# One q unit instead of two in the first stage, and another split of the modulation steps between VectorE and TensorE

## The chip, the core and the metric

The kernel runs on one core of one Trainium2 chip. The metric is the device time of one execution in microseconds (us); a kernel's time is the median of its runs. Beside the runs there is one profiled execution, whose trace all views of the profile come from. PE is TensorE (matmuls), PEld its weight loads, DVE is VectorE, ACT ScalarE, POOL GpSimd, SP the engine that issues most DMAs.

## The reference, cut to what matters

One layer of a diffusion backbone on 384 tokens (128 of context, 256 latent), model width 2048, everything in float32:

```python
mod = silu(cond) @ w_ada + b_ada              # 2048 -> 6 * 2048
sh1, sc1, ga1, sh2, sc2, ga2 = split(mod, 6)
h = rmsnorm(x, norm_pre_mix) * (1 + sc1) + sh1
proj = h @ w_in          # q 512 | k 512 | v 1024 | output gate g 1024 | lr 32 | Fourier 1024
o = bidirectional gated linear attention of q, k, v, log_sigmoid(lr @ w_a2 + b), 4 heads
o = rmsnorm(o) * gla_out_norm * silu(g)
f = real(fft2(Fourier groups))
gates = sigmoid(h @ w_gate + b_gate)          # 2048 -> 4096
m = (g_a * (o @ w_br_gla) + g_b * (f @ w_br_four)) @ w_out
x = x + ga1 * rmsnorm(m, norm_post_mix)
h = rmsnorm(x, norm_pre_ffn) * (1 + sc2) + sh2
x = x + ga2 * rmsnorm((silu(h @ w_ffn_gate) * (h @ w_ffn_up)) @ w_ffn_down, norm_post_ffn)
```

`cond` is one vector for the context tokens and one for the latent ones, so `mod` is a product of a 2048 x 12288 matrix with two vectors.

## The kernel before, in words

**Exact products.** A float32 product is made of three passes in a faster format: each operand is split into a high part (`hi`, a cast on ScalarE) and the rest (`lo`, a subtraction on VectorE), and a product is hi\*hi + hi\*lo + lo\*hi. Tokens stand along the free dimension, channels on the 128 partitions: an activation is 16 tiles of 128 x 384. A weight comes in pieces of 128 x 1024 (512 KB, tile `raw`, loaded by SP), which `split` (L264) turns into `whi` and `wlo`; in most stages one such piece is a **granule**: 8 k-tiles x 3 passes = 24 matmuls of 128 x 384 (`gemm`, L322, its matmul L326). One output tile of 128 channels over 2048 inputs takes two granules (`proj`, L348). `grab` (L313) takes the oldest split weight and splits the next; about three are held ahead, in four buffers each of `whi` and `wlo`. Every engine but SP runs in the order in which the program issues its work; nothing is reordered.

**Stage A (L406 to L660).** Sixteen steps `kb`, one per k-tile of h. A step makes the first two parts of the modulation for its channels (`gemv`, L470, 16 products with two 1 MB pieces `slab` of w_ada), normalises and modulates x to h, and adds the k-tile's contribution to all of v, which is summed in six PSUM banks (`vprod`, L482, 18 matmuls of 128 x 512). It also adds the contribution to the first `XU` = 2 units of q (a unit is 128 channels): `xprod` (L506) makes three matmuls of 128 x 384 per unit into a bank (`px`, and for unit 1 the bank `pgm` of the gemv), and `flush` (L500) adds the bank to an accumulator in SBUF on VectorE. Their weights come as `xraw` (`w_x`, 128 x 256, 128 KB a step) and are split by `split_w` (L428). SP's order in a step is: the two slabs of step kb+1, `raw` of v, `xraw`. Slabs have five buffers, `raw` and `xraw` two.

**Projections (L747 to L1000).** `qk_order` (L159) is k0, k1, then the q units that stage A has not made (q1 is made in stage A when XU is 2), then k2, k3: the first is `proj` with modulation steps alone beside it, the others with `side()`. Then come `GF` = 25 units of the merge gates. After each granule `side()` runs one step of the attention generator `gla()` and one **modulation step**. `gla` treats the heads one after another; a head is 14 steps (a step ends at a `yield`), of which one for each direction makes the exponentials and `qi`, `ki`, `ko` (L830 to L868) and the next makes the products `at` (L875) from them. Head 0 has three empty steps more.

**Modulation steps.** Three of the other four parts of the modulation are made by `ada_rest` (L685), in six groups of 18 steps: 16 k-steps, one empty step, and one that sums over partitions on TensorE (L718); the rest of that one (`ada_tail`, L665: two transposes and a few small VectorE operations) runs at the start of the next group's first k-step. A k-step has POOL load 512 KB (`adaw`, two buffers) and then multiplies it by the two conditioning columns: on VectorE with two operations of 128 x 1024 into `adacc` (L707, or L705 in a group's first), or, if `on_pe[0]` is set, on TensorE with eight matmul instructions into a bank `pr` (L697), called a TensorE granule of the modulation.

**Output gates and branches (L1000 to L1310).** After the Fourier projections comes `mix_order`: eight output-gate units `o` (two granules each, then `gcol`, L1193), the Fourier branch units `b` (`four`, L1225; one behind the third `o`, then one between the granules of each further `o` and one behind it), then sixteen branch units `a` of the attention branch (one granule each, from L1282) with five `b` among them. A `b` needs its weights folded by two VectorE operations (`fold`, L239) ahead of the cast and the subtraction. In the output gates `side()` (L1179) is called after each granule; call it turn 0 to 15. In before a modulation step is made at turns 0 to 8, 9, 11, 13, 15, on TensorE from turn 7 on but for turn 8. Ahead of the branch units `a` in `TAIL` (L41) one step is made, on TensorE where the entry is True. VectorE makes for each `a` the two merge operations L1296 and L1297 and the split of the one before (L379). The stage after, the output projection (L1350), needs all sixteen.

**The rest.** The output projection with the last steps of `ada_rest`, two norms, and the FFN with the last part of the modulation, where pieces of 128 x 512 are multiplied (L338), take from 733 us to the end.

The lines that set the modulation steps in the output gates and the branch units:

```python
on_pe[0] = turn[0] > 6 and turn[0] != 8      # side(), L1181
if turn[0] < 9 or turn[0] % 2:
    next(ada_gen, None)
...
if i in TAIL:                                # branch unit a, L1286
    on_pe[0] = TAIL[i]
    next(ada_gen, None)
```

Of the kernel before, what the change touches and what calls it, by code (L numbers as in the profile page):

```python
# [25 lines left out]
T = TC + TL  # L26
# [8 lines left out]
FC = 4  # L35
NFC = FT // FC
G = 1024
XU = 2
GF = 25
GD = 256  # L40
TAIL = {1: True, 4: False, 5: True, 8: True, 10: False, 11: True, 13: True, 14: False, 15: False}  # L41


C_TRI = 0
# [63 lines left out]
def tile_step(ctx: ExitStack, tc: tile.TileContext, a, o):  # L108
# [302 lines left out]
    with ExitStack() as s:  # L411
# [54 lines left out]
        pgm = pss.tile([P, 512], F32, tag="side", name="pgm")  # L466
        pgv, pmod = pgm[:, 0:256], pgm[:, 256:512]
        px = pss.tile([P, T], F32, tag="side", name="px")
# [10 lines left out]
        def passes(w):  # L479
            return ((0, w[0]), (0, w[1]), (1, w[0]))  # L480
# [25 lines left out]
        def xprod(u, kb, w, bank=px):  # L506
            def mm():
                for j, (x_, w_) in enumerate(passes(w)):
                    PE.matmul(bank, w_[:, u * P : (u + 1) * P], hT[x_][:, kb, :], start=j == 0, stop=j == 2)  # L509

            return mm, lambda dst=None: flush(xacc[u], kb == 0, dst, bank)
# [38 lines left out]
        prev = None  # L550
        for kb in range(KT):
            if kb and kb + 1 < KT:
                load_slab(kb + 1)
                load_w(kb + 1)
                if kb == 4:
                    load_later()

            wait = kb in (1, 2)
            if kb and not wait:
                gemv(kb)  # L560
            todo = []
            if kb > 4 and kb % 4 == 2:
                todo.append(lrprod(kb - 6))

            both = kb > 2
            if both:
                xs = [xprod(u, kb - 1, prev[1], bank) for u, bank in enumerate((px, pgm[:, 0:T]))]
            elif kb:
                todo += [xprod(u, kb - 1, prev[1]) for u in range(XU)]
            todo += [None] * (4 - len(todo))  # L570
            flushes = [t[1] if t else lambda: None for t in todo]

            def pe_x(n):
                if todo[n]:
                    todo[n][0]()

            if wait:
                vprod(kb - 1, prev[0], (0,))
            pe_x(0)
            hf = scr[:, kb % 8, :]  # L580

            xr = hf if kb else qs[0]
            DVE.tensor_mul(xr, xn(kb), rstd if kb else px)
            flushes[0]()
            if wait:
                gemv(kb)
            if kb:
                ev = pb.tile([P, 256], F32, tag="ev", name="ev")
                ACT.copy(ev, pgv)
            lag = []  # L590
            new = split_w(kb, lag)
            if kb:
                vprod(kb - 1, prev[0], (1 if wait else 0,))
            for m in range(2):
                PE.transpose(pmod[:, m * P : (m + 1) * P], ev[:, m * P : (m + 1) * P], ident)
            if kb == 0:

                for _ in range(6):
                    PE.matmul(pv[5][:, 0:P], ones, ones, start=True, stop=True)
            pe_x(1)  # L600

            pm = pb.tile([P, 2, 2], F32, tag="pm", name="pm", bufs=2)
            DVE.tensor_reduce(
                pm, pmod.rearrange("p (m q r) -> p m r q", m=2, q=4)[:, :, 0:2, :], axis=mybir.AxisListType.X, op=ALU.add,
            )
            DVE.tensor_scalar(
                mods[:, 1, kb, :], pm[:, 1, :], bsc1[:, 0, kb : kb + 1], norms[:, 0, kb : kb + 1],
                op0=ALU.add, op1=ALU.mult,
            )
            DVE.tensor_scalar_add(mods[:, 0, kb, :], pm[:, 0, :], cols[:, 0, kb : kb + 1])  # L610
            for lo, hi, c in segs:
                DVE.tensor_scalar(
                    hf[:, lo:hi], xr[:, lo:hi], mods[:, 1, kb, c : c + 1], mods[:, 0, kb, c : c + 1],
                    op0=ALU.mult, op1=ALU.add,
                )
                if kb == 0:
                    ACT.activation(
                        hT[0][:, kb, lo:hi], xr[:, lo:hi], AF.Identity,
                        bias=mods[:, 0, kb, c : c + 1], scale=mods[:, 1, kb, c : c + 1],
                    )  # L620
            flushes[1]()
            if kb:
                split_act(hT[0][:, kb, :], hT[1][:, kb, :], hf)
            else:
                ACT.copy(rstd, px)
                DVE.tensor_sub(hT[1][:, kb, :], hf, hT[0][:, kb, :].bitcast(F32))
            if kb:
                if not wait:
                    vprod(kb - 1, prev[0], (1,))
                pe_x(2)  # L630
                flushes[2]()
            if both:
                for mm, _ in xs:
                    mm()
                for _, fl in reversed(xs):
                    fl()
            for sub in lag:
                sub()
            if kb:
                vprod(kb - 1, prev[0], (2,))  # L640
                pe_x(3)
                flushes[3]()
            prev = new
# [109 lines left out]
    with ExitStack() as s:  # L753
# [25 lines left out]
        def gla():  # L779
# [10 lines left out]
            for h in range(NH):  # L790
# [38 lines left out]
                for d in range(2):  # L829


                    bT = pss.tile([P, T], F32, tag="side", name="bT")
                    for t in range(3):
                        for j, l in enumerate((lah, lal)):
                            PE.matmul(
                                bT[:, t * P : (t + 1) * P], l[:, t, d], tri[:, d * P : (d + 1) * P],
                                start=j == 0, stop=j == 1,
                            )
                    sx = pss.tile([P, 2, P], F32, tag="side", name="sx")
                    for j, l in enumerate((lah, lal)):  # L840
                        PE.matmul(
                            sx, tri[:, (2 + d) * P : (3 + d) * P], l[:, 0 : 2 + d : 1 + d, d], start=j == 0, stop=j == 1,
                        )
                    eb = pg.tile([P, T], F32, tag=f"eb{d}", name="eb")
                    ACT.activation(eb, bT, AF.Exp)
                    ki = pg.tile([P, T], F32, tag=f"ki{d}", name="ki")
                    ACT.activation(ki, bT, AF.Exp, scale=-1.0)
                    ko = pg.tile([P, 2, P], F32, tag=f"ko{d}", name="ko")
                    ACT.activation(ko, sx, AF.Exp)
                    qi = pg.tile([P, T], F32, tag=f"qi{d}", name="qi")  # L850
                    DVE.scalar_tensor_tensor(qi, eb, DK**-0.5, qT[:, h, :], op0=ALU.mult, op1=ALU.mult)
                    DVE.tensor_mul(ki, ki, kT[:, h, :])
                    DVE.tensor_mul(ko, ko, krs[:, 0 : 2 + d : 1 + d, :])

                    last = 0 if d else CH - 1
                    tot = chunks(eb)[:, :, d, last : last + 1]
                    kc = pg.tile([P, 3, CH], F32, tag=f"kc{d}", name="kc")
                    DVE.tensor_mul(kc, chunks(ki)[:, :, d, :], tot.to_broadcast([P, 3, CH]))
                    dc = pg.tile([P, 1], F32, tag=f"dc{d}", name="dc")
                    c = 5 if d else 2  # L860
                    e0, e1 = c * CH + last, (c + 1 - 2 * d) * CH + last
                    DVE.tensor_mul(dc, eb[:, e0 : e0 + 1], eb[:, e1 : e1 + 1])
                    qin.append(qi)
                    kin.append(ki)
                    kcr.append(kc)
                    kout.append(ko)
                    dec.append((tot, dc))
                    yield  # L868

                ats = []  # L870
                for d in range(2):
# [33 lines left out]
                ap = [apt[:, 0], apt[:, 1]]  # L905
                split_act(*ap, att)
                yield
                qpt = [pg.tile([P, 2, 3, P], F32R, tag=t, name="qp") for t in ("lah", "lal")]
                qp = [[q[:, d] for q in qpt] for d in range(2)]
                for d in range(2):  # L910
# [88 lines left out]
    px = fs.enter_context(tc.tile_pool(name="px", bufs=1))  # L999
# [93 lines left out]
    with ExitStack() as s:  # L1093
# [83 lines left out]
        turn = [0]  # L1177

        def side():  # L1179
            while True:  # L1180
                on_pe[0] = turn[0] > 6 and turn[0] != 8  # L1181
                if turn[0] < 9 or turn[0] % 2:
                    next(ada_gen, None)
                on_pe[0] = False
                turn[0] += 1
                next(df, None)
                next(nw, None)
                yield
# [121 lines left out]
    with ExitStack() as s:  # L1310
# [94 lines left out]
        u = pd.tile([P, 2, 3], F32, name="u12", bufs=1)  # L1405
# [355 lines left out]
        bank = {}  # L1761
# [69 lines left out]
        for kind, c, i in steps[:-4]:  # L1831
# [8 lines left out]
            if kind == "D":  # L1840
# [9 lines left out]
                h = hid_last if last_c else hid  # L1850
# [248 lines left out]
```

## Time and profile before

| what | us |
|---|---|
| median of 3 runs | 1943.53 (1941.89 to 1943.78) |
| profiled execution, device time | 1942.28 |
| profiled execution, span from first to last instruction | 1940.4 |

About 1.9 us lie around the span. TensorE's granted clock was 0.998 of full speed over the span. In the profile page the first part gives the busy time of each engine, the second the span in 40 slices, the fourth the chain of work that ended last; the groups, the waits, the windows and the timeline are views of the same trace that can be asked for a stretch of it. A time such as 612.53 is us from the span's start. A matmul's end is modelled and overlaps the next one's start, so the cost of a run of matmuls is read from start to start.

### The profile page before, as it was taken

How to read it: one execution, taken by the hardware profiler on the slowest of the kernel's cores; microseconds unless marked ns; L12 is line 12 of the kernel's file. 1: busy time of each engine (PE TensorE's matmuls, PEld its weight loads, DVE VectorE, ACT ScalarE, POOL GpSimd, SP SyncE). 2: the span in 40 equal slices, each digit the busy share in tenths (PEclk: the TensorE clock that was granted, in tenths of full speed). 3: DMA queues.
4: the chain of work that ended last, by engine and by line, in shares of the span. 5: the costliest groups of instructions: out<-in, count | busy, mean ns of one | idle time of the engine just before them, and what ended most of it. 6: DMA issues, size and time to landing. Idle time of an engine off the chain costs nothing.

```text
span 1940.4 us, 27538 instructions
## 1 busy us (share of the span) xinstructions
PE 1920.4 (99%) x10534; PEld 1690.8 (87%) x10534; DVE 1647.8 (85%) x2172; ACT 916.3 (47%) x1298; POOL 85.8 (4%) x154
## 2 busy tenths in 40 slices
PE   9999999999999999999999999999999999999997
PEld 5779999999999999999988888888888888888886
DVE  5668898889878887978789888999998999888885
ACT  4235455545456554456455444444444444444444
POOL 0001111100000000104000000000000000000001
PEclk9999999999999999999999999999999999999999
DMA  9977766766757885755264636363636272625243
GB/s 390 387 260 248 240 234 227 248 231 194 225 185 246 302 302 181 245 193 198 83 195 131 200 103 194 121 211 98 216 104 213 91 222 93 201 76 185 87 173 110
DMA packets 200615, 380.52 MB, mean 196 GB/s; under 512 B 14196, under 2 KB 126932, under 8 KB 196132
## 3 DMA queue, kind: packets, MB, share of 16 engines
q1 hardware_dynamic: 181252, 320.84, 48.9%
q0 software_dynamic: 13952, 50.39, 8.5%
q10 hardware_dynamic: 5280, 7.55, 1.1%
q8 instruction: 82, 1.34, 0.3%
q14 instruction: 49, 0.40, 0.1%
HBM read 361.94 MB, written 16.78 MB: 195 GB/s over the span
## 4 chain that ended last, share of the span: by engine, by line
PE 93%; DVE 3%; DMA 2%; issue 1%; ACT 1%; SPq 0%; DVEq 0%; ACTq 0%
PE pgu L338 30%; PE pmm L326 30%; PE pdn L338 18%; PE pv L491 3%; PE pgm L474 1%; PE pf L1239 1%; PE pfo L1039 1%; DVE adacc L707 1%; PE pmm L1516 1%; PE ptr L1808 1%; PE pf L1240 1%; PE pfo L1040 1%; DMA xraw<-in_w_x 1%; PE po L788 1%; PE px L509 0%
## 5 line engine op out<-in xcount | busy, mean ns | idle before, releaser
L326 PE MATMUL pmm<-A_hi,whi 128*128 128x384 f32 x1072 | 361.7, 337 | 0.0
L326 PE MATMUL pmm<-A_hi,wlo 128*128 128x384 f32 x1072 | 358.8, 335 | 0.0
L326 PE MATMUL pmm<-A_lo,whi 128*128 128x384 f32 x1072 | 358.6, 335 | 0.0
L1663 ACT CAST whi<-u 128x1024 fp32r<-128x1024 f32 x200 | 210.6, 1053 | 281.5 <-DVE u L1647 86.5
L1663 ACT CAST whi<-raw 128x1024 fp32r<-128x1024 f32 x175 | 184.2, 1052 | 200.8 <-PE pgu L338 63.8
L1674 DVE TENSOR_TENSOR wlo<-u,whi 128x1024 fp32r<-128x1024 f32 x200 | 244.1, 1220 | 32.0 <-ACT whi L1663 18.3
L338 PE MATMUL pgu<-whi,A_hi 128*128 128x512 f32 x640 | 250.0, 391 | 0.0
L338 PE MATMUL pgu<-whi,A_lo 128*128 128x512 f32 x640 | 249.3, 389 | 0.0
L1674 DVE TENSOR_TENSOR wlo<-raw,whi 128x1024 fp32r<-128x1024 f32 x175 | 213.4, 1220 | 34.6 <-ACT whi L1663 25.6
L287 DVE TENSOR_TENSOR wlo<-raw,whi 128x1024 fp32r<-128x1024 f32 x163 | 198.2, 1220 | 24.1 <-ACT whi L300 23.7
L300 ACT CAST whi<-raw 128x1024 fp32r<-128x1024 f32 x149 | 156.0, 1051 | 117.6 <-PE pmm L326 50.0
L326 PEld LDWEIGHTS pmm<-A_hi,whi 128*128 128x128 f32 x1072 | 201.2, 188 | 3.3 <-issue 2.5
L326 PEld LDWEIGHTS pmm<-A_lo,whi 128*128 128x128 f32 x1072 | 201.4, 188 | 0.2
L326 PEld LDWEIGHTS pmm<-A_hi,wlo 128*128 128x128 f32 x1072 | 201.2, 188 | 0.3 <-DVE wlo L287 0.2
L707 DVE SCALAR_TENSOR_TENSOR adacc<-adaw,spad,adacc 128x1024 f32<-128x1024 f32 x160 | 198.1, 1279 | 3.5 <-DMA adaw<-in_w_ada 3.2
L338 PE MATMUL pdn<-whi,hid_hi 128*128 128x512 f32 x480 | 186.9, 389 | 0.0
L338 PE MATMUL pdn<-whi,hid_lo 128*128 128x512 f32 x480 | 186.8, 389 | 0.0
L338 PE MATMUL pgu<-wlo,A_hi 128*128 128x512 f32 x640 | 184.2, 389 | 0.0
L338 PEld LDWEIGHTS pgu<-whi,A_hi 128*128 128x128 f32 x640 | 120.2, 188 | 26.1 <-issue 0.8
L338 PEld LDWEIGHTS pgu<-wlo,A_hi 128*128 128x128 f32 x640 | 120.1, 188 | 25.4
L338 PEld LDWEIGHTS pgu<-whi,A_lo 128*128 128x128 f32 x640 | 120.1, 188 | 25.0
L338 PE MATMUL pgu<-whi,S 128*128 128x512 f32 x480 | 131.1, 395 | 0.0
(405 smaller groups left out, 3042.7 us busy)
## 6 DMA issues: line engine op xcount, KB each, us to landing
adaw<-in_w_ada POOLq DMA_DIRECT2D x96, 512.0 KB, 4.0
raw<-in_w_d SPq DMA_DIRECT2D x88, 512.0 KB, 3.7
slab<-in_w_ada SPq DMA_DIRECT2D x32, 1024.0 KB, 10.2
raw<-in_w_gate SPq DMA_DIRECT2D x64, 512.0 KB, 4.4
raw<-in_w_g SPq DMA_DIRECT2D x48, 512.0 KB, 3.4
raw<-in_w_u SPq DMA_DIRECT2D x48, 512.0 KB, 3.5
raw<-in_w_in SPq DMA_DIRECT2D x44, 512.0 KB, 4.3
u<-in_w_u SPq DMA_DIRECT2D x40, 512.0 KB, 4.6
```

The lines of the kernel that those rows point to most:

```text
L287: eng.tensor_sub(lo, raw, hi.bitcast(F32))
L300: ACT.copy(hi, raw)
L326: PE.matmul(dst, w[wi][:, k * n + n0 : k * n + n0 + P], x[xi][:, k0 + k, :], start=first and k == 0 and j == 0, stop=last and k == kts - 1 ...
L338: PE.matmul(dst, stat[x_][m], mov(w[w_], m), start=first and w_ == m == x_ == 0, stop=last and w_ == m == 1,)
L474: PE.matmul(pgv[q : q + 32, :], spad[:, k, :], slab[k // (KT // 2)][:, k % (KT // 2), :], start=k < 4, stop=k >= KT - 4,)
L491: PE.matmul(pv[2 * t + g], hT[x_][:, kb, t * P : (t + 1) * P], w_[:, g * 512 : (g + 1) * 512], start=kb == 0 and j == 0, stop=kb == KT - 1 ...
L707: DVE.scalar_tensor_tensor(acc[:, c, :], w, spad[:, k, c : c + 1], acc[:, c, :], op0=ALU.mult, op1=ALU.add,)
L788: PE.matmul(dst, w[wi], x[xi], start=first and j == 0, stop=last and j == 2)
L1039: PE.matmul(p, w_of[0][:, i, k, g, :], x[:, :, lo:hi], start=kt == 0, stop=False)
L1040: PE.matmul(p[:, 0], w_of[1][:, i, k, g, :], x[:, 0, lo:hi], start=False, stop=kt == KT - 1)
L1663: ACT.copy(hi, src)
L1674: DVE.tensor_sub(lo, src, hi.bitcast(F32))
```

## The change

```diff
-XU = 2
+XU = 1
-TAIL = {1: True, 4: False, 5: True, 8: True, 10: False, 11: True, 13: True, 14: False, 15: False}
+TAIL = {1: False, 3: False, 5: False, 7: False, 8: False, 10: False, 13: False, 14: False, 15: False}
...
-                xs = [xprod(u, kb - 1, prev[1], bank) for u, bank in enumerate((px, pgm[:, 0:T]))]
+                xs = [xprod(u, kb - 1, prev[1], bank) for u, bank in enumerate((px, pgm[:, 0:T])[:XU])]
...                                              # gla(), after the loop that makes qi, ki, ko
+                if h == 0:
+                    yield
...                                              # gla(), after the splits of att
+                if h == 0:
+                    yield
...                                              # side() of the output gates
-                if turn[0] < 9 or turn[0] % 2:
+                if turn[0] < 7 or turn[0] in (8, 9, 13, 15):
                     next(ada_gen, None)
```

Stage A makes one unit of q; its `xraw` is 128 x 128. The unit q1 becomes one more `proj` in the projections, behind k1: two granules, two calls of `side()`. Head 0 of the attention gets two more empty steps, one ahead of `at` and one ahead of the products of the new states. The number of modulation steps up to the end of the branch units is the same (87): two more beside the projections, two fewer in the output gates, nine in the branch units as before. With the two steps more ahead of them, the steps of the generator fall on other turns: turns 3 and 4 become the empty step and the sum of a group, turn 5 the tail and the next group's first k-step, turns 6 and 8 its second and third. On TensorE are turns 9, 13 and 15 alone (five in the output gates and five in the branch units before); VectorE makes all nine steps in the branch units (four before). From the output projection on nothing differs.

## The prediction

> **What bounds the kernel now.** I read the page's busy times and chain first, then the busy time of each engine by stage.
>
> ```profile
> PE 1920.4 (99%) x10534; PEld 1690.8 (87%) x10534; DVE 1647.8 (85%) x2172; ACT 916.3 (47%) x1298; POOL 85.8 (4%) x154
> PE 93%; DVE 3%; DMA 2%; issue 1%; ACT 1%; SPq 0%; DVEq 0%; ACTq 0%
> ```
>
> ```profile
> core 0: us, PE busy (x) PEld busy (x) DVE busy (x) ACT busy (x) POOL busy (x), PEclk, DMA share, GB/s
> 44.00:128.00 84.00, 84.00 (x662) 60.45 (x661) 52.86 (x125) 23.62 (x44) 0.00 (x0) 1.00 0.96 366
> 160.00:195.00 35.00, 33.45 (x227) 33.03 (x226) 33.95 (x39) 21.72 (x30) 3.96 (x8) 1.00 0.68 233
> ...
> 583.00:657.00 74.00, 74.00 (x493) 70.31 (x486) 63.57 (x131) 49.08 (x74) 3.17 (x6) 1.00 0.79 257
> 657.00:727.00 70.00, 70.00 (x436) 66.87 (x435) 60.67 (x108) 35.63 (x62) 3.68 (x7) 1.00 0.90 313
> ```
>
> TensorE makes the time: it is busy in 99% of the span, and 93% of the chain is PE. So an edit is worth the matmul time that it takes away, plus the stalls of TensorE that it ends, less those that it makes. The windows say where new ones threaten. In stage A (44 to 128) TensorE has no gap, but the DMA engines are busy for 0.96 of the time as well. Where the first attention head runs (160 to 195), VectorE is the busier engine, 33.95 of 35 us, and TensorE misses 1.55 us. In the output gates (583 to 657) and the branch units (657 to 727) VectorE is busy for 63.57 of 74 and 60.67 of 70 us: it is a close second, and the change sends it work there.
>
> **Stage A gives up one unit of q.** These are pieces of the chain, start and length:
>
> ```profile
> 26.33 0.23 PE pgm L595 x2
> ...
> 28.03 0.52 ACT A_hi L378
> ...
> 105.65 1.86 PE pgm L474 x32
> ...
> 111.23 0.52 PE pgm L509 x3
> ...
> 113.14 1.86 PE pgm L474 x32
> ```
>
> ```profile
> 242.50 8.32 PE pmm L326 x48
> ```
>
> A step takes 113.14 - 105.65 = 7.49 us, without a gap. Unit 1 (`pgm`) is 0.52 of it, so 16 steps give 16 x 0.523 = 8.4 us. Its 48 matmuls come back as two granules in the projections, 8.32 us there (8.35 with the change of granule). On matmuls alone the move is worth nothing. I take two amounts off the gain. Step 1 does not get shorter: from its transposes (26.33) to the cast (28.03) that TensorE waits for runs a chain of small VectorE operations, and the dropped unit lies beside it, 0.5 us. The other amount is in the transfers:
>
> ```profile
> 20.00:40.00 20.00, 19.51 (x158) 12.71 (x157) 12.59 (x28) 6.72 (x13) 0.00 (x0) 1.00 1.02 415
> ```
>
> ```profile
> slab<-in_w_ada SPq DMA_DIRECT2D x26, 1024.0 KB, 9.8
> raw<-in_w_v SPq DMA_DIRECT2D x14, 512.0 KB, 5.8
> ```
>
> ```profile
> 60.13 0.61 PEld L474 LDWEIGHTS pgm<-slab,spad 128*32 128x32 f32 x16 [0.25 <-DMA slab<-in_w_ada]
> ```
>
> With `xraw`, 128 KB by the code, a step reads 2 x 1024 + 512 + 128 KB = 2.75 MB, afterwards 2.69 MB. At the 415 GB/s of the window from 20 to 40 us that is 6.63 and 6.47 us against 7.49 and 6.97 us of TensorE: in the steady state TensorE stays the bound. The start does not have that room. At 60.13 (step 6) the weight load waits 0.25 us for its slab, so this slab lands just in time; by then TensorE is to be four shorter steps earlier (2.1 us), the transfers only 5 or 6 x 0.16 us. I take a stall of 1.2 us. Stage A: -8.4 + 0.5 + 1.2 = **-6.7**, between -8.4 (no wait) and -2.5 (16 x 64 KB at 415 GB/s: the transfers as the bound throughout). I take a value nearer the first end because the wait at 60.13 is no longer than 0.25 us and ends within its step. With the two granules: **+1.7** (0 to +5.9).
>
> The Trainium skill, "DMA: Bandwidth & Descriptors", section Specifications, gives about 358 GB/s as the HBM limit of one core; by it a step of 2.69 MB could not take less than an estimated 7.5 us, stage A would gain nothing, and the sum below would be some 7 us higher. The row above shows 415 GB/s, so the trace does not agree, and that case stands only as a rival, on its own rows.
>
> **The first head.** Its products `at` wait for VectorE.
>
> ```profile
> PEld at L875 <- issue: 1.7, 1, 1.7
> PE at L875 <- DVE ki L852: 1.5, 1, 1.5
> ```
>
> With the new empty step a granule of 4.2 us lies between `ki` and `at`, while VectorE needs only one more modulation step and one subtraction, 2.4 + 1.1 us (rows below). The stall goes: **-1.7** (end to end 0, if it comes back at another wait for VectorE, which is then 1.7 us further behind). Next is the subtraction `wlo` of the granules, which has granules in hand.
>
> **Seven modulation steps go from TensorE to VectorE.** First TensorE, two starts that follow each other:
>
> ```profile
> 590.58 0.64 PE L697 MATMUL pr<-adaw,spad 128*32 128x256 f32 x8
> 591.15 0.55 PE L1196 MATMUL pt<-ident,qk 128*128 128x128 f32 x3
> ```
>
> A step costs TensorE 0.57 us; seven fewer are 4.0 us. Two of the seven land beside the projections, where a granule of 8.32 / 2 = 4.16 us leaves room for a step and a subtraction of VectorE, 2.4 + 1.1 us: nothing to pay, but up to 2.4 us of lag if the head's own work fills that room. Five come into the branch units. Now VectorE:
>
> ```profile
> 586.39 1.23 DVE L287 TENSOR_TENSOR wlo<-ws,whi 128x1024 fp32r<-128x1024 f32 x1 [1.11 <-ACT whi L294]
> ...
> 591.80 0.23 DVE L676 COPY mods<-ptm 128x8 f32<-128x8 f32 x2
> ...
> 592.33 0.61 DVE L1199 SCALAR_TENSOR_TENSOR gs<-gs,gnorm,pt 128x384 f32<-128x384 f32 x1
> ...
> 599.88 1.41 DVE L705 TENSOR_SCALAR adacc<-adaw,spad 128x1024 f32<-128x1024 f32 x2
> 601.21 1.22 DVE L287 TENSOR_TENSOR wlo<-ws,whi 128x1024 fp32r<-128x1024 f32 x1
> ```
>
> ```profile
> 675.46 2.47 DVE L707 SCALAR_TENSOR_TENSOR adacc<-adaw,spad,adacc 128x1024 f32<-128x1024 f32 x2
> 677.85 0.68 DVE L243 TENSOR_TENSOR ws<-raw 128x512 f32<-128x512 f32 x1
> ```
>
> From start to start a step costs 677.85 - 675.46 = 2.39 us, a group's first 601.21 - 599.88 = 1.33, the tail 592.33 - 591.80 = 0.53. What VectorE has more to do from turn 5 to the last branch unit: at turn 5 tail and first step stand ahead of an output gate, whose other operands come later by the sum that turn 4 now makes on TensorE, and push it back some 1.2 us (an estimate from 0.53, 1.33 and the sum's 1.0); at turn 6 a step, of which 1.11 fills the wait at 586.39: 1.28; at turn 7 the tail is gone: -0.53; at turn 8 a full step in place of a first one: 1.06; in the branch units nine steps for four: 5 x 2.39 = 11.95. Together **15.0 us**. Against it stands VectorE's idle time, of which only that spent waiting for TensorE can be used up:
>
> ```profile
> DVE wlo L287 <- ACT whi L294: 6.6, 9, 1.2
> ```
>
> ```profile
> DVE gate L1296 <- PE pmm L326: 8.5, 9, 1.5
> ```
>
> The first is the output gates (583 to 657): VectorE waits there for casts of its own results, and these waits move with it. The second is the branch units (657 to 728): 8.5 us that it can use. So its last split for the branch units comes 15.0 - 8.5 = 6.5 us later. When is it needed?
>
> ```profile
> 736.47 1.23 DVE L379 TENSOR_TENSOR A_lo<-yb,A_hi 128x384 fp32r<-128x384 f32 x2
> ```
>
> ```profile
> 737.58 0.33 PE L326 MATMUL pmm<-A_hi,whi 128*128 128x384 f32 x1
> ```
>
> It ends at 737.7. The output projection's second granule starts with k-tile 8 at 737.58 and gets to k-tile 15 after 21 matmuls of 8.32 / 48 = 0.173 us, at 741.2: 3.6 us in hand. TensorE gets there 6.5 - 3.6 = 2.9 us later than now instead of 4.0 earlier. I take **+2.8**: the saving is lost and more. The ends are -4.0 (VectorE is never waited for) and +6 (the late merges also hold PSUM banks, and late subtractions hold the `raw` buffers that SP must refill, as it already waits for VectorE there).
>
> **The sum.** +1.7 - 1.7 + 2.8 = +2.8 us. On the profiled execution, 1942.3 (span 1940.4 and 1.9 around it), that is 1945.1; this execution is 1.2 below the median of the runs, so I set the sum on the median: 1943.5 + 2.8, or **1946** rounded down. A measurement of this kernel can tell about 0.2%, 3.9 us, from no change.
>
> **The rivals.**
> *VectorE hides it all* (faster). The lead of the granules and the idle time carry the nine steps, and stage A gains in full: -8.4 + 8.35 - 1.7 - 4.0 = -5.8, 1938. For it: TensorE waits for VectorE hardly anywhere now. Against it: 15.0 us of work on 8.5 us of idle time and 3.6 us in hand.
> *Stage A is bound by transfers* (slower). If TensorE's shorter step meets DMA engines that cannot go faster, the step shrinks only by its bytes, 2.5 us over the stage: +5.9 - 1.7 + 2.8 = +7, 1950.5. It decides once 2.69 MB take longer than 6.97 us, below 386 GB/s. For it: a DMA share of 0.96 and 366 GB/s; against it: 415 GB/s in the stretch where the transfers set the pace.
> *A lagging VectorE costs more than its own work* (slower): banks and `raw` buffers as above, +6 in place of +2.8: 1949.5.
> *The stall of head 0 only moves* (it does not do what it says): +4.5, 1948.
>
> **Chances.** Forecast 0.50, its own range 1943 to 1949 (0.40 of it within 3.9 us, 0.10 above); VectorE hides it 0.13 (0.11 faster, 0.02 same); transfers 0.17 (slower); more lag 0.15 (0.11 slower, 0.04 same); moved stall 0.05 (0.03 same, 0.02 slower). Faster 0.11, same 0.49, slower 0.40. For 8 in 10 the range leaves out most of the first rival and the upper half of the transfers': 1940 to 1950.5.
>
> **What would show it.** Right: steps of 6.97 us in stage A with one longer wait for a slab near step 6; no wait of `at` for `ki`; no idle time of VectorE before L1296 from 660 to 725, and waits of TensorE for `wlo` or `A_lo` between 595 and 745 of 6 to 7 us in all. Wrong: steps near 7.4 us (transfers), or TensorE without a gap up to 745 (VectorE hides it). Past 745 both kernels do the same, and a difference there would be none of these.

## The result and the profile after

The changed kernel takes 1945.23 us (median of 22 runs, 1943.46 to 1946.31), the kernel before 1942.61 us beside it (22 runs, 1941.39 to 1944.13). The ratio is 1.0013 with a 95% interval of 1.0007 to 1.0019: 2.6 us slower (1.4 to 3.7), less than the 0.2% named in the prediction. The profiled execution took 1945.94 us, its span is 1944.2 us.

The engines' busy times and the chain, from the page of the changed kernel:

```profile
PE 1918.4 (99%) x10478; PEld 1690.7 (87%) x10478; DVE 1655.8 (85%) x2172; ACT 915.6 (47%) x1301; POOL 85.8 (4%) x154
PE 81%; DVE 8%; DMA 5%; ACT 2%; issue 2%; SPq 0%; ACTq 0%; DVEq 0%
```

TensorE has 2.0 us less to do than before, yet the span is longer: VectorE's part of the chain grew from 3% to 8%, that of DMA from 2% to 5%. The windows that were read before show where (columns as there: busy time of PE, PEld, DVE, ACT, POOL, then clock, DMA share and GB/s):

```profile
44.00:128.00 84.00, 83.19 (x671) 58.01 (x664) 48.66 (x121) 23.95 (x47) 0.00 (x0) 1.00 0.93 360
160.00:195.00 35.00, 35.00 (x237) 34.68 (x236) 33.41 (x38) 19.06 (x26) 4.47 (x10) 1.00 0.67 235
583.00:657.00 74.00, 72.88 (x465) 69.76 (x464) 64.91 (x125) 47.14 (x72) 2.64 (x5) 1.00 0.73 235
657.00:727.00 70.00, 66.67 (x389) 66.02 (x388) 69.18 (x117) 35.92 (x62) 3.17 (x6) 0.98 0.90 302
```

Stage A has a gap of 0.8 us of TensorE. The gap of the first head (1.55 us before) is gone. In the output gates TensorE misses 1.1 us and in the branch units 3.3 us, where it missed nothing before, and VectorE, which had 9.3 us without work in the branch units, is now busy in 69.18 of 70 us.

**Stage A.** The chain in the steady part, start and length of each piece:

```profile
108.66 1.86 PE pgm L474 x32
110.53 1.58 PE pv L491 x6
112.11 0.22 PE pgm L595 x2
112.33 1.39 PE pv L491 x6
113.72 0.52 PE px L509 x3
114.25 1.39 PE pv L491 x6
115.63 1.86 PE pgm L474 x32
```

A step takes 115.63 - 108.66 = 6.97 us, with TensorE alone in the chain: unit 1 is gone from it, and no transfer has taken its place. At step 6 a transfer does: the weight load for the second half of the gemv waits for its slab, 1.29 us in the place of 0.25. (At step 3, 37.36 us, it waits 0.98 us in the place of 0.23.)

```profile
59.31 0.59 PEld L474 LDWEIGHTS pgm<-slab,spad 128*32 128x32 f32 x16 [1.29 <-DMA slab<-in_w_ada]
```

**Output gates and branches.** The waits of TensorE from 595 to 745 us, in all, times, longest:

```profile
PE pf L1244 <- DVE wlo L287: 4.5, 4, 1.9
```

All four are at Fourier units (`b`), whose folded weights need two VectorE operations more than others before the subtraction. The lag is thus paid there, and not, as forecast, at the output projection. The last splits for the branch units:

```profile
742.60 1.22 DVE L379 TENSOR_TENSOR A_lo<-yb,A_hi 128x384 fp32r<-128x384 f32 x2
```

742.60 against 736.47 before. In this execution TensorE is late enough by then not to wait for them.

One thing in this trace was in no forecast, the clock right behind the longest of the four waits:

```profile
705.00:706.00 1.00, 0.99 (x4) 0.99 (x5) 1.00 (x1) 0.00 (x0) 0.00 (x0) 0.65 0.94 322
706.00:708.00 2.00, 2.00 (x9) 2.00 (x9) 1.97 (x5) 0.82 (x2) 0.00 (x0) 0.50 0.92 322
708.00:709.00 1.00, 1.00 (x7) 1.00 (x6) 1.00 (x2) 1.00 (x3) 0.00 (x0) 0.65 0.79 268
```

The granted clock is 0.50 from 706 to 708 and, by 0.65 in the windows beside it, for 0.7 us more on either side: 3.4 us at half rate, which cost TensorE 1.7 us.

### The profile page after: what moved, and what is told of

The parts are those of the page before. It is cut to its first block, busy times and chain, and to the rows that moved or that the text cites. A ratio compares the mean times of both kernels' runs of the same rounds, so it can differ in the third digit from the quotient of the medians.

```text
span 1944.2 us, 27444 instructions
## 1 busy us (share of the span) xinstructions
PE 1918.4 (99%) x10478; PEld 1690.7 (87%) x10478; DVE 1655.8 (85%) x2172; ACT 915.6 (47%) x1301; POOL 85.8 (4%) x154
## 4 chain that ended last, share of the span: by engine, by line
PE 81%; DVE 8%; DMA 5%; ACT 2%; issue 2%; SPq 0%; ACTq 0%; DVEq 0%
PE pgu L338 29%; PE pmm L326 25%; PE pdn L338 17%; PE pv L491 2%; DMA slab<-in_w_ada 2%; DVE adacc L707 2%; DVE wlo L287 1%; DMA raw<-in_w_in 1%; PE pgm L474 1%; PE pfo L1043 1%; PE pmm L1520 1%; DVE wlo L1678 1%; DMA raw<-in_w_g 1%; ACT whi L300 1%; PE ptr L1812 1%
## 5 line engine op out<-in xcount | busy, mean ns | idle before, releaser
L326 PE MATMUL pmm<-A_hi,whi 128*128 128x384 f32 x1088 | 366.8, 337 | 0.0
L326 PE MATMUL pmm<-A_hi,wlo 128*128 128x384 f32 x1088 | 364.2, 335 | 0.5 <-DVE wlo L287 0.5
L326 PE MATMUL pmm<-A_lo,whi 128*128 128x384 f32 x1088 | 363.9, 334 | 0.0
L707 DVE SCALAR_TENSOR_TENSOR adacc<-adaw,spad,adacc 128x1024 f32<-128x1024 f32 x174 | 215.4, 1280 | 3.7 <-DMA adaw<-in_w_ada 3.3
```

The source lines that it names most:

```text
L326: PE.matmul(dst, w[wi][:, k * n + n0 : k * n + n0 + P], x[xi][:, k0 + k, :], start=first and k == 0 and j == 0, stop=last and k == kts - 1 ...
L707: DVE.scalar_tensor_tensor(acc[:, c, :], w, spad[:, k, c : c + 1], acc[:, c, :], op0=ALU.mult, op1=ALU.add,)
```

## The experiments

All times are medians beside runs of the kernel before on the same chip; the latter had medians of 1942.5 to 1942.7 us. A difference of medians is known to about 1.7 us, so the small terms are read from the traces, by the start of the same instruction in each.

### The changed kernel again

No edit.

> The changed kernel once more, in another execution. Three things of its first trace are to be told apart: what belongs to the change and what to one execution. Theory: the waits of TensorE for folded branch weights (L1244 for wlo, 4.5 us between 595 and 745) recur, as does the wait for a slab near step 6 of stage A; VectorE is busy without a gap from 660 to 737 (76.18 of 77 us in the first trace). Rival: the half-rate stretch of TensorE's clock behind the 1.86 us wait at 705 (0.50 between 706 and 708), the 0.64 us wait at 521 and the later 0.8 us in the FFN belong to the change too, and recur. I expect these three to be absent or elsewhere, and 2 to 3 us over the kernel before as the time; with all of them again it would be 3.7.

Measured: 1945.15 us against 1942.51 (+2.6; ratio 1.0014, 1.0005 to 1.0023), span 1942.2 us. Its waits of TensorE from 595 to 745 us:

```profile
PE pf L1244 <- DVE wlo L287: 4.4, 4, 1.8
PE pmm L326 <- DVE A_lo L379: 0.8, 1, 0.8
```

and the branch units in it, with the last splits (the first row is a window):

```profile
660.00:737.00 77.00, 73.67 (x435) 73.02 (x435) 76.14 (x122) 35.66 (x62) 4.22 (x8) 1.00 0.90 302
```

```profile
741.76 1.22 DVE L379 TENSOR_TENSOR A_lo<-yb,A_hi 128x384 fp32r<-128x384 f32 x2
```

The waits at the Fourier units recur, so does that for the slab (1.6 us). The clock stays at 1.00 this time, although the same wait, 1.85 us, precedes: the half-rate stretch belongs to an execution. Two more runs below execute the changed program from the projections on and have the same wait of 1.85 us at this place: with more bytes the clock falls (0.50 from 720 to 722 us), with the small loads later it does not. The wait at 521 is absent too. And with TensorE 1.7 us earlier, the forecast wait at the output projection is there: TensorE waits 0.8 us for `A_lo` at k-tile 14 (741.2 us). From the last merge gate to the FFN this execution takes 412.0 us, the one with the half rate 412.3; the other two take 411.8 us without and 412.3 with it. So most of the 1.7 us that the clock took away, TensorE would otherwise have spent waiting for VectorE, which sets the end of this stretch.

### TAIL of before on the changed kernel

```diff
-TAIL = {1: False, 3: False, 5: False, 7: False, 8: False, 10: False, 13: False, 14: False, 15: False}
+TAIL = {1: True, 4: False, 5: True, 8: True, 10: False, 11: True, 13: True, 14: False, 15: False}
```

> The changed kernel with TAIL of before: five of the nine modulation steps in the branch units are on TensorE again, everything else as changed. Theory (VectorE's work sets the branch units): VectorE has 15.0 - 11.95 = 3.05 us more to do than before against 8.5 us of usable idle time, so the waits for folded weights at 686 and 703 go and VectorE waits for TensorE in the branch units again; the waits at 598 to 627 (1.6 us in all, ahead of any step of TAIL) stay. Against before: +1.7 - 1.7 - 1.1 (two steps fewer on TensorE) + 1.6 = +0.5 us, some 2 us under the changed kernel. First rival (the waits in the output gates are made up later): -1.1. Second rival (the loss is not in the branch units): five steps of 0.57 us more on TensorE and no wait less, changed kernel + 2.9, +5.5 against before.

Measured: 1942.99 us against 1942.51 (+0.5; ratio 1.0003, 0.9994 to 1.0012). Waits of TensorE from 595 to 745, then of VectorE from 657 to 741:

```profile
PE pf L1244 <- DVE wlo L287: 1.1, 2, 0.7
```

```profile
DVE gate L1300 <- PE pmm L326: 4.9, 4, 1.5
```

The theory's number, though the interval (-1.2 to +2.3 us) would hold the first rival's as well; the trace decides. VectorE again waits for TensorE in the branch units, and the two waits at 612 and 627 us, ahead of any step of `TAIL`, stay. From the last merge gate to the FFN this kernel takes 410.7 us, 0.6 more than the kernel before: two steps fewer on TensorE give 1.35 us, and the two waits take 1.94 us from start to start, 0.8 more than the idle time in the row. So the rest of the loss lies in the five steps, and more than the two steps of the output gates save is lost in the output gates themselves.

### Six on VectorE, three on TensorE

```diff
-TAIL = {1: False, 3: False, 5: False, 7: False, 8: False, 10: False, 13: False, 14: False, 15: False}
+TAIL = {1: True, 3: False, 5: True, 7: False, 8: True, 10: False, 13: False, 14: False, 15: False}
```

> The changed kernel with three of the nine steps in the branch units on TensorE (units 1, 5, 8), six on VectorE. Theory: VectorE has 15.0 - 3 x 2.39 = 7.8 us more to do than before, which the 8.5 us of usable idle time just hold; its last split for the branch units comes no later than before, TensorE keeps 4 of the 7 saved steps (2.3 us). Against before: 0 - 2.3 + 1.6 (the waits at 598 to 627) = -0.7 us, the fastest of the three splits. Rival (what costs is each late subtraction, not the sum of VectorE's work): waits at the Fourier units stay in part, 1 to 2 us, and the time is that of before or up to +1.3.

Measured: 1943.15 us against 1942.51 (+0.6; ratio 1.0003, 0.9994 to 1.0012). The time does not tell it from the run before. In the trace no wait of TensorE for VectorE is left between 628 and 745 us, and from the last merge gate to the FFN it takes 409.2 us, 0.9 less than the kernel before (410.1) and 1.5 less than with `TAIL` of before (410.7), as the theory has it; but a wait of 0.8 us at 521 us, which is ahead of the edit, and two waits in the FFN's last pieces near 1890 us (1.3 us, 0.4 in the kernel before) took the gain away. The trace speaks for the theory; the time leaves it open.

### Nine on VectorE, on the kernel before

```diff
-TAIL = {1: True, 4: False, 5: True, 8: True, 10: False, 11: True, 13: True, 14: False, 15: False}
+TAIL = {1: False, 3: False, 5: False, 7: False, 8: False, 10: False, 13: False, 14: False, 15: False}
```

> The kernel before with one edit alone: TAIL of the change, nine steps in the branch units on VectorE in place of four. Theory by the sum of VectorE's work: 11.95 us more against 8.5 us of idle time, so its last split comes 3.45 us later, 741.2 instead of 737.7, and TensorE, 2.85 us ahead of before at that place (5 x 0.57), waits for it until the time at which it is there now: no difference, 0 (-0.5 to +0.5). Rival one (VectorE hides the five steps): -2.85. Rival two (the five steps bring the whole loss of the change, by waits at the Fourier units that add up): +2 to +3.

Measured: 1941.74 us against 1942.51 (-0.8; ratio 0.9992, 0.9983 to 1.0001). TensorE's waits from 595 to 745, and the last splits:

```profile
PE pf L1240 <- DVE wlo L287: 1.4, 1, 1.4
PE pmm L326 <- DVE A_lo L379: 0.8, 1, 0.8
```

```profile
739.20 1.22 DVE L379 TENSOR_TENSOR A_lo<-yb,A_hi 128x384 fp32r<-128x384 f32 x2
```

```profile
L1296 DVE TENSOR_TENSOR gate<-gate,pmm 128x384 f32<-128x384 f32 x16 | 8.8, 549 | 0.0
```

The last row is a group of VectorE from 657 to 741 us; its last number is the idle time ahead of it, 8.5 us before and none now. So the five steps used up 8.5 us and made the last splits 739.20 - 736.47 = 2.7 us later: 11.2 us, 2.24 us a step and not the 2.39 of the row in the prediction. The 0.75 us between these 2.7 and the 3.45 us of the expectation is the size of the miss from 0 to -0.8. By the medians alone -0.8 is not told from 0 (-3.3 to +0.2 us); the trace has 409.35 us from the last merge gate to the FFN against 410.14. Nine steps are a small gain here, and a loss in the change, since there VectorE comes to the branch units 2.6 us later (its first merge at 659.6 in the second execution of the changed kernel, 656.9 before).

### An empty step of head 0 alone

```diff
                     dec.append((tot, dc))
                     yield
+                if h == 0:
+                    yield
```

> The kernel before with one empty step of head 0 ahead of the products at, nothing else. Theory: at no longer waits 1.5 us for ki and the time of the first head falls by 1.7 us, -1.7 against before; by this the unit of q moved out of stage A is worth +1.7 of the change's 0 up to the end of the projections. Rival (the wait only moves to another product of the same head, or to the end of the attention, where one step more is drained behind the projections): 0.

Measured: 1944.19 us against 1942.73 (+1.5; ratio 1.0008, 0.9999 to 1.0017). The theory's -1.7 falls; a loss by the medians is likely, not certain (-0.2 to +3.3 us). No wait of `at` is left, but these came; TensorE's waits from 140 to 445 us, then from 445 to 480:

```profile
PE dl L788 <- DVE part L379: 0.4, 1, 0.4
PE bT L835 <- DVE lal L379: 0.4, 1, 0.4
```

```profile
PE pmm L326 <- DVE wlo L287: 1.5, 1, 1.5
```

The attention now has one step more than before, and the calls of `side()` are the same 60: at the end of the projections three steps are drained at once instead of two, VectorE does them ahead of the next subtraction, which starts at 445.84 us where it started at 444.27, and TensorE waits for a later one at 458 us. The change does not have this wait: q1 brings two granules and so two calls more for its two empty steps. That is the cover under which the stall of head 0 could go.

The other half of the miss is the size of that stall. The kernel before and the two kernels that differ from it only behind 650 us are three executions of one program there:

```profile
PE at L875 <- DVE ki L852: 1.5, 1, 1.5
```

```profile
PE at L875 <- DVE ki L852: 0.7, 1, 0.7
```

```profile
PE at L875 <- DVE ki L852: 0.3, 1, 0.3
```

(the kernel before, nine steps, eight steps). With the pause around the wait that is 1.7, 0.9 and 0.5 us: the first trace showed the largest.

### Eight on VectorE, on the kernel before

```diff
-TAIL = {1: True, 4: False, 5: True, 8: True, 10: False, 11: True, 13: True, 14: False, 15: False}
+TAIL = {1: False, 3: False, 5: False, 7: False, 8: True, 10: False, 13: False, 14: False, 15: False}
```

> The kernel before with eight steps in the branch units on VectorE in place of four (unit 8 alone on TensorE). The run with nine gave -0.8 us, with VectorE's work 11.2 us longer up to its last split, 2.23 us a step. Theory by the sum: 4 x 2.23 = 8.9 us more against 8.5 us of idle time and 3.6 us in hand, so the last split comes in time and TensorE keeps 4 x 0.57 us: -2.3. Rival (each late subtraction of a Fourier unit counts by itself): a wait of 1 to 1.6 us at the Fourier unit near 700 stays, as with nine, and the time is -0.7 to -1.3.

Measured: 1939.99 us against 1942.73 (-2.7; ratio 0.9989, 0.9980 to 0.9998). It beats both kernels. The window of the branch units:

```profile
657.00:727.00 70.00, 70.00 (x421) 69.34 (x420) 69.21 (x113) 34.84 (x60) 3.69 (x7) 1.00 0.91 316
```

TensorE has no gap and VectorE almost none. From the last merge gate to the start of the output projection it takes 195.6 us, 198.6 before: 3.05 us for four steps, 0.76 each and not 0.57. Where the rest comes from, the starts around such a step of the kernel before show:

```profile
692.79 0.34 PE L326 MATMUL pmm<-o_hi,wlo 128*128 128x384 f32 x1
693.06 0.64 PE L697 MATMUL pr<-adaw,spad 128*32 128x256 f32 x8
693.62 0.45 PE L326 MATMUL pmm<-o_hi,whi 128*128 128x384 f32 x1
693.91 0.34 PE L326 MATMUL pmm<-o_lo,whi 128*128 128x384 f32 x1
694.09 0.35 PE L326 MATMUL pmm<-o_hi,wlo 128*128 128x384 f32 x1
```

From 692.79 to 694.09 three matmuls at 0.173 us would take 0.52 us; with the step it is 1.30. The step costs 0.78: the matmul ahead of it and the one behind it are 0.10 and 0.12 us longer from start to start, which the row used for the forecast (from the step's first start to the next) left out.

### Both edits together

```diff
+                if h == 0:
+                    yield                  # ahead of at
...
+TAIL = {1: False, 3: False, 5: False, 7: False, 8: True, 10: False, 13: False, 14: False, 15: False}
```

> The two edits together, the empty step of head 0 and eight steps on VectorE, on the kernel before, with two units of q in stage A. Theory: the terms lie in different stages and add up, -1.7 - 2.3 = -4.0 us. Rival: one of them is given back at a later wait, -1.7 to -2.3.

Measured: 1942.18 us against 1942.73 (-0.6; ratio 0.9999, 0.9991 to 1.0008). 2.2 us more than with eight steps alone: the wait of 1.5 us at 458 is there again, and one of 1.1 us at 521. Within what the medians can tell the terms do add up, but that of the empty step is a loss.

### The empty step moved, not added

Two kernels, each with eight steps on VectorE and the empty step ahead of `at`, and one of the other three empty steps of head 0 taken away: one of the two behind the splits of `la`, or the one ahead of `z`.

```diff
                 if h == 0:
                     yield
-                    yield                  # the first kernel, behind the splits of la
...
-                if h == 0:                 # the second kernel, ahead of z
-                    yield
```

> The kernel before with eight steps in the branch units on VectorE, and in head 0 one of the two empty steps behind the splits of la moved to the place ahead of at, so that the attention has as many steps as before. Theory: the wait of at for ki (0.5 to 1.7 us in the three executions of this program up to there) goes, and with no step added at the end of the attention the wait of 1.7 us near 458 does not come: about 1 us under the run with eight steps alone, -3.7 against before. Rival: the sums bT of head 0, now one granule earlier, wait for lal, and the gain is given back: -2.7 or less of a gain.

> As the run with the moved empty step, but the step taken away is the empty one at the start of head 0, ahead of the product z. Theory: the same, -3.7 against before, no wait of at for ki and none near 458. Rival: z or the splits of la, one granule earlier, wait instead: -2.7 or less of a gain.

Measured: 1940.32 us against 1942.48 (-2.2; 0.9986, 0.9977 to 0.9995) and 1941.33 us (-1.1; 0.9991, 0.9982 to 0.9999), neither under the 1939.99 of the eight steps alone (-2.7 beside its own runs of the kernel before). For the first the interval, -4.5 to -1.0 us, still holds the theory's -3.7; the traces decide. TensorE's waits from 140 to 445 us, one row of each:

```profile
PE dl L788 <- DVE part L379: 1.3, 1, 1.3
```

```profile
PE z L808 <- ACT krs L796: 1.3, 1, 1.3
```

`at` waits no longer and the end of the attention is as before, but now the products of the states wait for a split, or `z` for ScalarE's copy of `krs`. The rival is right, at another place than it had named in the first kernel: with as many granules as before, head 0's stall was moved, and not ended, by both places tried.

### More bytes in stage A

```diff
             SP.dma_start(xraw[kb], a["w_x"][kb])
+            more = pb.tile([P, G], F32, tag="more_x", name="more_x", bufs=1)
+            SP.dma_start(more, a["w_gate"][kb, 0])
```

> The changed kernel with 512 KB more read in every step of stage A (a piece that nothing uses), 3.19 MB a step in place of 2.69 MB. Theory: stage A has room in its transfers, whose limit is near the 415 GB/s of the window from 20 to 40 us; 3.19 MB take 7.7 us there, so the steady step grows from 6.97 to about 7.7 us and the stage by 9 to 11 us. First rival (the transfers are the bound of the changed stage already, at 2.69 MB in 6.97 us, 386 GB/s): every byte counts, steps of 8.3 us, 18 to 21 us more. Second rival (the limit is far above 415 GB/s): steps stay below 7.2 us, less than 4 us more.

Measured: 1959.44 us, one run, 14.2 us over the changed kernel. Starts of gemv steps, and a window over five of them:

```profile
112.68 1.07 PE L476 MATMUL pgm<-slab,spad 128*32 128x256 f32 x16
...
120.43 1.07 PE L476 MATMUL pgm<-slab,spad 128*32 128x256 f32 x16
122.07 1.07 PE L476 MATMUL pgm<-slab,spad 128*32 128x256 f32 x16 [0.57 <-DMA slab<-in_w_ada]
```

```profile
89.00:128.00 39.00, 36.40 (x284) 24.43 (x283) 20.83 (x52) 10.15 (x20) 0.00 (x0) 1.00 1.02 413
```

The steady step is 120.43 - 112.68 = 7.75 us, with a wait for a slab in each, at 413 GB/s and a DMA share of 1.02: the theory's 7.7 us. So the limit of the transfers is where the window from 20 to 40 us showed it, and the changed stage, with 2.69 MB in 6.97 us (386 GB/s), lies under it. The Trainium skill ("DMA: Bandwidth & Descriptors", section Specifications) gives about 358 GB/s for one core, as half of what two cores share; with the one core that runs here, this run does not agree with that figure as a limit. The stage grew by 13.5 us, more than the 9 to 11 expected: steps 1 to 6 lost 8.6 of these. The start had no room; besides, the clock was 0.50 from 68 to 70 us behind a wait of 2.1 us, and the added piece has one buffer, so that SP waited for it (24.4 us in all from 40 to 130 us). What each of the three cost is not separated.

### Four small loads later

```diff
         def load_later():
             SP.dma_start(wlr, a["w_lr"])
+
+        def load_last():
             SP.dma_start(coef[:, 0:2], a["consts"][:, C_COEF : C_COEF + 2])
             ...
                 if kb == 4:
                     load_later()
+                if kb == 12:
+                    load_last()
```

> The changed kernel with four small loads (53 KB in all: coef, bgate, gnorm, selr) issued at step 12 of stage A instead of step 4; only the 256 KB of wlr stay at step 4. In the trace of the changed kernel the transfers fall to 115 to 314 GB/s for some 3 us near 50 us, with 911 packets under 512 bytes from 40 to 75 us, at a DMA share of 0.9 and more, and step 6 waits 1.3 us for its slab. Theory: these packets, not the bytes of the slabs, cause that wait; it goes, stage A ends 1.1 us earlier and the time is that of the changed kernel - 1.1 (+1.5 against before). Rival (the 256 KB or the shorter steps cause it): the wait stays at 1 us and the time is that of the changed kernel.

Measured: 1944.19 us against 1942.48 (+1.7; ratio 1.0009, 1.0000 to 1.0017), 1.0 under the changed kernel, which the medians alone can't tell from nothing. In the trace the wait at step 6 is gone (0.3 us is left at step 4, 44.4 us) and the projections start 1.1 us earlier, at 134.7. Two microseconds at the small loads, in the changed kernel and here (last columns DMA share and GB/s):

```profile
50.00:51.00 1.00, 1.00 (x15) 0.46 (x17) 1.00 (x2) 0.00 (x0) 0.00 (x0) 1.00 0.83 227
51.00:52.00 1.00, 1.00 (x26) 0.56 (x20) 1.00 (x3) 0.00 (x0) 0.00 (x0) 1.00 0.81 160
```

```profile
50.00:51.00 1.00, 1.00 (x15) 0.47 (x17) 1.00 (x2) 0.00 (x0) 0.00 (x0) 1.00 1.08 422
51.00:52.00 1.00, 1.00 (x24) 0.60 (x20) 1.00 (x3) 0.00 (x0) 0.00 (x0) 1.00 1.11 451
```

With the 53 KB in small packets the rate is about half and less while the share stays above 0.8. The wait at step 6 is theirs. But slow packets are not the only way in which they can cause it. SP issues the two slabs of step 6 behind the small loads, in the changed kernel and here (start, length):

```profile
50.44 1.65 SPq L419 DMA_DIRECT2D slab<-in_w_ada  x2
```

```profile
45.87 0.86 SPq L419 DMA_DIRECT2D slab<-in_w_ada  x2
```

In the changed kernel SP waited for earlier transfers to land ahead of them:

```profile
SPq L419 <- DMA slab<-in_w_ada: 2.2, 1, 2.2
SPq L419 <- DMA raw<-in_w_v: 0.9, 1, 0.9
```

Each was the transfer issued eight before: in this stretch SP has no more than eight under way, and four small loads take four of these places, whatever their size. So the slabs also came late into the queue, 4.6 and 5.4 us later than here. The run moves both causes at once and can't say which share is whose. At step 12, where the loads are now, the rate falls to 140 and 182 GB/s from 105 to 107 us, and TensorE does not wait: by then there is room. The Trainium skill ("DMA: Bandwidth & Descriptors", section Specifications) gives 512 bytes as the least size of a transfer for full rate; the rows go that way, but do not separate it from the late slabs.

## Why the prediction was right, point by point

The stretches of the kernel, in the executions that have the same program there. "Before's program" up to the last merge gate is the kernel before and the runs with nine and eight steps on it, "the changed program" the changed kernel, the same again, and it with `TAIL` of before and with three on TensorE. The marks are the first `pmm` matmul, ScalarE's evictions of the 25th and of the last merge gate, and the first FFN matmul.

| stretch, us | before's program | changed program | difference of means |
|---|---|---|---|
| stage A | 142.3, 142.6, 142.4 | 135.7, 135.9, 135.9, 135.8 | -6.6 |
| to the 25th merge gate | 297.0, 296.2, 295.8 | 303.6, 303.4, 303.4, 303.3 | +7.1 |
| to the last merge gate | 95.5, 96.1, 95.5 | 96.3, 95.5, 95.5, 96.6 | +0.3 |
| to the FFN | 410.1 | 412.3, 412.0 | +2.0 |
| FFN | 995.5, 995.6, 996.8 | 996.3, 995.5, 995.7, 996.6 | 0.0 |

The sum is +2.8 us, beside +2.6 by the medians; the forecast was +2.8 and 1946 us, and 1945.2 came. That the sum is so close is in part luck: its terms missed by +0.4 and +0.3 ahead of the last merge gate and by -0.8 behind it, and these cancel.

- **Stage A, -6.7 by the forecast:** right in sum, with steps of 6.97 us and a wait near step 6. What was taken off the gain, 0.5 + 1.2 us, came otherwise: about 0.2 at step 1, 0.7 at step 3, which the forecast did not have, and 1.0 at step 6. The cause was only half right. The start has no room, as said, but what fills it at step 6 are the four small loads and not the shorter steps alone: without them the wait is gone with steps as short.
- **Two granules, +8.35, and the first head, -1.7:** +7.1 measured, 6.65 forecast. The stall does go, but it was taken from one execution; the mean of three is 1.0 us (1.7, 0.9, 0.5). And it goes without a new wait only because the new granules pay for the empty steps, as the four kernels without them show; the forecast had not seen this as a condition. Alone, the empty step cost 1.5 us by the medians.
- **Seven steps to VectorE, +2.8:** +2.0 measured (412.3 and 412.0 against 410.1). The mechanism is as forecast: VectorE is the bound of the branch units, and without a half-rate stretch TensorE waits at k-tile 14 of the output projection. The two prices were off. A step costs TensorE 0.76 us, not 0.57 (seven: 5.3 in place of 4.0), and VectorE 2.24, not 2.39. VectorE's last split was to come 6.5 us later; it comes 5.3 later in the undisturbed execution, 2.6 (forecast 15.0 - 11.95 = 3.05) at its first merge, 11.2 for five steps, less 8.5 of idle time. Less 3.6 in hand that is +1.7, near the measured +2.0. TensorE's own saving does not enter, as VectorE sets the end.
- **Where TensorE waits:** 6 to 7 us between 595 and 745 were forecast, 5.2 us of idle time are measured in the second execution (4.4 and 0.8). A wait costs more than its idle time: from start to start the Fourier products take 5.7 us more than in the kernel before and the stretch from the output projection to the FFN 1.3 us more, 7.0 in all. Less the 5.1 us by which the seven steps and their neighbours are shorter in these two traces, that is the +1.8 of this execution. The forecast had put the waits at the output projection and given the Fourier units' weights no price; most of them fall there. By the forecast's own reasoning that moves no time, since whichever wait comes first takes from the later ones; no run tests this.
- **"Past 745 both kernels do the same":** right for the program, but not a check that one trace can make: the FFN alone takes 995.5 to 996.8 us in three executions of before's program, and 996.3 and 995.5 us in the two of the changed kernel. Of the 3.7 us between the first two traces, 0.8 us is of that kind. Not all of it need be chance: in all five kernels with six or eight of the nine steps on VectorE the FFN takes 996.5 to 996.9 us, so a part of what they gain ahead of it is lost in it. Why stays open.
- **The rivals:** transfers as the bound of stage A are excluded by the run with more bytes; VectorE hiding it all by the two runs with nine steps. "The stall of head 0 only moves" is true of the four kernels tried without the two granules.

Why the wait at 521 us (0 to 1.1 us) comes in some executions and not in others, of either program, stays open; so does why two executions lost their clock behind the same wait and two did not.

## What to carry to other kernels

When one engine is made to help another, the gain runs up to the point at which both have no gap, and ends there: here eight steps on VectorE gave 2.7 us, nine on the same kernel 0.8 (by the trace), and nine with 2.6 us of other work moved to it cost time. Price an operation by what the stretch loses with it, from the neighbour ahead to the neighbour behind, and take a stall's size from more than one execution. And before a slot is inserted into a schedule that runs beside other work, count whether the other work has a slot more to give: the end of the schedule pays otherwise.

## What the hardware showed beyond that

- A wait of TensorE of 1.85 us at the same place of the program was followed by 3.4 us at a granted clock of 0.50 in two of four executions (the changed kernel and the run with more bytes) and not in the others (the changed kernel again, the run with later loads). The Trainium skill ("TensorE: Matmul & The Clock Gate", section Part 1: The HAM clock gate) has the clock halved after an idle window of some 3.4 us; here a wait little more than half as long was enough, twice in four traces.
- While four small transfers, 53 KB in all, were under way, the 16 DMA engines moved 160 to 227 GB/s for two microseconds in which they otherwise moved 422 to 451 GB/s. The 1 MB pieces behind them were issued 4.6 and 5.4 us later, as SP had no more than eight transfers under way, and stage A ended 1.1 us later.
